# A two-layer mLSTM and windowed-attention trunk: filling order and rotation sums in attention, and the mLSTM gate chain, selectors, conditioning steps and latent squares, changed together

## The chip, the cores and the metric

The kernel runs on one core of a Trainium2 chip. A core has TensorE (PE in the profile; PEld is its weight load), VectorE (DVE), ScalarE (ACT), GpSimd (POOL) and SyncE (SP, which issues most DMAs here). Each engine works through its own instructions in order and waits for the others by semaphores. The metric is the time of one execution in microseconds (us) on the device.

## What is computed

Two layers of a trunk over 512 latent tokens and 256 context tokens, with 1024 features and float32 throughout. Both layers are modulated by linear maps of a conditioning vector (`mod_l`, `mod_c`). The reference, cut:

```python
for i in range(2):                      # layer 0: bidirectional mLSTM, layer 1: windowed attention
    mod_l = split(silu(c) @ ada_w[i] + ada_b[i], 6)      # mod_c the same from c_ctx
    u  = rms_norm(h,  norm_mix[i]) * (1 + mod_l[1]) + mod_l[0]      # uc from hc likewise
    y, yc = mlstm(uc, u) if i == 0 else attention(uc, u)
    h = h + mod_l[2] * y
    h = h + mod_l[5] * (relu(modulated_norm(h) @ w1[i]) ** 2 @ w2[i])
    # layer 0 does the same for the context stream hc
return rms_norm(h, final_norm)
# mlstm: gates -> log_i, log_sigmoid(log_f); per direction, in 128-token chunks:
b = cumsum(lf); m = running max of (m + lf, li); weights exp(...) from b, li, m
# attention: rope(q), rope(k); scores to 3 neighbouring blocks of 128 and to the context; softmax with a sink
```

## The kernel before

Every float32 product is made of three TensorE products (`mm3`, lines 93 to 98): each operand is split into a rounded part (`hi`, a copy on ACT, line 876) and the rest (`lo`, a subtraction, line 877, on DVE unless another engine is named). Weights come in units of 512 KB through a ring with three raw buffers (`unit`, line 74); `take` and `feed` keep the next ones ready.

The program is written with a tile framework. Its planner orders each engine's instructions by their place in the program and by when it reckons them ready, and places the waits. `keep_in_program_order` pins one instruction behind whatever was written before it for its engine. Fillers are Python generators: each `next` writes a few more instructions of other work at that place.

Layer 0. `layer0_mix` makes the gate logits and the first queries and keys. `gates` (line 576) is one generator: the chain of logarithms, four scans and three exponentials on DVE, ACT and POOL is written at its first `next`, ahead of `qk_out` and the values of the first head pair (`v_steps`, line 686); the second half, transposes on TensorE, follows after one and a half blocks of the output gate (`ogate`). Then `core` (line 725) runs for four head pairs, with the next pair's projections as filler. `new_es` (line 718) spreads selector columns for one pair; its product at line 740 begins a core, with the scaled keys `kp` (line 753). `ada_step` (line 249) is one conditioning step: a raw unit is loaded and multiplied with one or two conditioning rows on DVE (line 261, pinned). 80 such steps are spread over the layers: in `dense_steps`, in `v_steps` at j = 5, 1 and 3 of the order 4, 5, 0, 1, 2, 3, and elsewhere.

End of the mixer and feed-forward network of layer 0. `out_late` adds the mixer's output to `hC` and `hL`; `norm_add` (line 279) squares each of the eight blocks on ACT and adds the squares up on POOL, the last two on DVE. `norm_hooks` gives two hooks: `norm_rc` (line 300, sums over partitions on TensorE at line 307, then a power on POOL) and the normalisation itself. `plain` in `ffn0` (line 1008) does the first four hidden blocks, context before latent, with the latent's hooks after the first two context blocks. In the last round, `back` (line 1089) takes one block at a time, each in a bank of the pool `mm` (three banks; `at` has five).

Layer 1. `keys_begin` projects the context's keys and values, with the hooks of the latent norm inside. `rope` (line 1664) makes a rotation from three DVE products and one POOL sum (line 1677); `kv_out` and `q_out` split the result, and their `late` part transposes it on TensorE (lines 1702 and 1719) and copies it out. The attention loop runs over 16 tiles (g, j). In each, the string `PAT` sets the order: S is a quarter of a later tile's scores (`scores`, line 1726), T a turn of weights (line 1793, evacuated at lines 1798 and 1799), V a product with the values, F one filler step. The fillers (line 1541) come in the order: the late parts of the tile before, four key-value projection steps, four query steps, output projections. They and the turns share the pool `pt` (three banks).

Of the kernel before, what the change touches and what calls it, by code (L numbers as in the profile page):

```python
# [9 lines left out]
F32 = mybir.dt.float32  # L10
# [11 lines left out]
P = 128  # L22
# [34 lines left out]
class Trunk:  # L57
# [222 lines left out]
    def norm_add(self, st, g, kt, h, eng=None, temp=None, apart=False):  # L280
# [5 lines left out]
        elif kt:  # L286
            sq = self.np.tile([P, n], F32, name="sq", tag=f"sq{n}", bufs=2)
        else:
            sq = self.np.tile([P, n], F32, name=f"ss{g}", tag=f"ss{n}", bufs=1 if n == 512 else 2)
# [10 lines left out]
    def norm_rc(self, st, g):  # L300
# [4 lines left out]
        for j in range(nb):  # L305
            for i, acc in enumerate(st[g]):
                nc.tensor.matmul(out=ps[:, j:j + 1], lhsT=acc[:, j * P:(j + 1) * P], rhs=self.ones, start=i == 0,
                                 stop=i == len(st[g]) - 1)
# [43 lines left out]
    def layer0_mix(self):  # L352
# [79 lines left out]
        with tc.tile_pool(name="ml", bufs=1, reuse_waits="tile") as ml:  # L432
# [81 lines left out]
    def out_late(self, yu):  # L514
# [23 lines left out]
        for g in "CL":  # L538
# [3 lines left out]
            for n, m in enumerate((6, 7, 0, 1, 2, 3, 4, 5)):  # L542
# [8 lines left out]
                self.norm_add(self.st, g, n, self.out_add(m, g, t), nc.vector if n > 5 else None)  # L551
# [5 lines left out]
    def norm_hooks(self, g):  # L557
# [9 lines left out]
        return [lambda: x.append(self.norm_rc(st, g)), whole]  # L567

    def gates(self, psc, psl):
# [21 lines left out]
        with tc.tile_pool(name="gt", bufs=1, reuse_waits="tile") as gt:  # L591
# [33 lines left out]
            nc.gpsimd.tensor_tensor(out=t1[R], in0=li, in1=b, op=ALU.subtract)  # L625
# [20 lines left out]
            nc.scalar.activation(out=az, in_=az, func=AF.Exp)  # L646
# [4 lines left out]
            nc.scalar.activation(out=t1[64:104], in_=aa, func=AF.Exp)  # L651
            nc.scalar.activation(out=t2, in_=m, func=AF.Exp, scale=-1.0)
# [34 lines left out]
    def v_steps(self, p, v, rows, w=None):  # L687
        w = w or [self.take() for i in range(2)]
        for j in (4, 5, 0, 1, 2, 3):
# [9 lines left out]
            if p and j % 2:  # L699
# [18 lines left out]
    def new_es(self, p):  # L718

        self.es = self.mc.tile([104, 2, P], F32R, name="es", tag="es", bufs=2)  # L720
# [204 lines left out]
    def ffn0(self, hooks, done, pre):  # L925
# [82 lines left out]
        def plain(hid):  # L1008

            ws = [self.begun.pop(0) for _ in range(4)]  # L1010
            pools = [("mm", self.mm)] * 3 + [("at", self.at)]
            for g in "CL":
                xs = self.xs(self.u0)
                for m in range(4):
                    hi, lo = ws[m]
                    n = xs[g](0)[0].shape[-1]
                    ps = pools[m][1].tile([P, 512], F32, name="mm", tag=pools[m][0])[:, :n]
                    for kt in range(KT):
                        sl = slice(kt * P, (kt + 1) * P)
                        self.mm3(ps, hi[:, sl], lo[:, sl], *xs[g](kt), kt == 0, kt == KT - 1)  # L1020
                    r = r_tile(n)
                    nc.scalar.activation(out=r, in_=ps, func=AF.Relu)
                    nc.scalar.activation(out=r, in_=r, func=AF.Square)
                    if g == "C":
                        self.split(r, *[x[:, P:H] for x in hid[m][1]])
                        if m < 2:
                            hooks[m]()
                    else:
                        self.split(r[:, 0:H], *hid[m][0])
                        self.split(r[:, H:NL], *[x[:, 0:P] for x in hid[m][1]])  # L1030
                        self.feed()
                        if m % 2:
                            blocks(m // 2)
                        if m == 1:
                            self.ada_until(0, 5)
# [53 lines left out]
        def back(c, todo, hid, w, late=False):  # L1089
# [30 lines left out]
        for _ in range(2):  # L1120
            self.feed(True)
# [851 lines left out]
```

## Time and profile before

| | us |
|---|---|
| time, median of 3 runs (1566.23 to 1571.36) | 1568.58 |
| profiled execution, its own time | 1573.33 |
| its span | 1571.5 |
| PE / PEld busy | 1519.8 / 1365.5 |
| DVE / ACT / POOL busy | 1123.5 / 744.2 / 341.3 |

The span runs from the first to the last instruction of the profiled execution. Matmuls overlap, so a busy TensorE is not one at its peak. [...]

### The profile page before, as it was taken

The numbers are of one execution on the slowest core, as the hardware profiler recorded it, in microseconds if no ns is written. First come the engines' busy times: TensorE is split into PE (matmuls) and PEld (weight loads), VectorE is DVE, ScalarE is ACT, GpSimd is POOL, SyncE is SP. The second block draws the span as 40 slices with busy tenths as digits, with TensorE's granted clock in tenths as the row PEclk, the third lists the DMA queues.
The fourth block names the chain that finished last, engine by engine and source line by source line (L and its number), as shares of the span: only waits on it lengthen the run. The fifth ranks groups of instructions, "written<-read, shape, count | busy, mean of one in ns | idle before, by whom it ended". The sixth has DMA issues, their size and how long they took to land.

```text
span 1571.5 us, 23851 instructions
## 1 busy us (share of the span) xinstructions
PE 1519.8 (97%) x9110; PEld 1365.5 (87%) x9110; DVE 1123.5 (71%) x2064; ACT 744.2 (47%) x1506; POOL 341.3 (22%) x333
## 2 busy tenths in 40 slices
PE   7989999999999999999999999899999999999998
PEld 5778888878889999999999999788887888888886
DVE  3666556478777797876776668777888785767687
ACT  4534343334473533424325255566666665545454
POOL 0221111112213222233223322354443100000000
PEclk9989999999999999999999999999999999999999
DMA  8323223234321343343443421011101424150321
GB/s 311 131 74 108 94 95 94 79 101 138 101 68 67 105 136 123 133 148 119 149 135 120 134 81 66 23 41 41 41 28 55 157 82 151 40 170 32 107 68 54
DMA packets 47849, 157.28 MB, mean 100 GB/s; under 512 B 5327, under 2 KB 8911, under 8 KB 47607
## 3 DMA queue, kind: packets, MB, share of 16 engines
q1 hardware_dynamic: 46560, 154.25, 29.4%
q8 instruction: 72, 1.18, 0.3%
q10 hardware_dynamic: 1175, 1.51, 0.3%
q14 instruction: 42, 0.34, 0.1%
HBM read 153.64 MB, written 2.10 MB: 99 GB/s over the span
## 4 chain that ended last, share of the span: by engine, by line
PE 71%; DVE 8%; issue 6%; POOL 5%; ACT 4%; DMA 1%; POOLq 0%; DVEq 0%; ACTq 0%
PE mm L96 16%; PE mm L97 16%; PE mm L98 16%; DVE adap L261 2%; PE p L98 2%; PE p L96 2%; PE p L97 2%; PE pt L1793 1%; PE pj L96 1%; PE pj L98 1%; PE pj L97 1%; DVE wlo L877 1%; PE at L832 1%; ACT whi L876 1%; PE av L1809 1%
## 5 line engine op out<-in xcount | busy, mean ns | idle before, releaser
L877 DVE TENSOR_TENSOR wlo<-raw,whi 128x1024 fp32r<-128x1024 f32 (+2 forms) x152 | 182.6, 1205 | 87.9 <-ACT whi L876 87.1
L876 ACT CAST whi<-raw 128x1024 fp32r<-128x1024 f32 (+2 forms) x155 | 154.0, 1000 | 139.1 <-PE mm L97 74.7
L96 PE MATMUL mm<-uH,whi 128*128 128x512 f32 (+1 forms) x496 | 191.4, 390 | 3.9 <-ACT v L698 3.9
L97 PE MATMUL mm<-uL,whi 128*128 128x512 f32 (+1 forms) x496 | 188.8, 382 | 0.4 <-DVE uL L331 0.4
L98 PE MATMUL mm<-uH,wlo 128*128 128x512 f32 (+1 forms) x496 | 188.9, 382 | 0.0
L261 DVE SCALAR_TENSOR_TENSOR adap<-raw,crow 128x1024 bf16<-128x1024 f32 x128 | 167.0, 1305 | 21.6 <-DMA raw<-ada 20.8
L96 PE MATMUL mm<-h,whi 128*128 128x384 f32 x512 | 173.7, 339 | 4.0 <-DVE hL L1110 2.2
L97 PE MATMUL mm<-h,whi 128*128 128x384 f32 x512 | 172.9, 338 | 0.5 <-DVE h L877 0.5
L98 PE MATMUL mm<-h,wlo 128*128 128x384 f32 x512 | 172.6, 337 | 0.0
L96 PEld LDWEIGHTS mm<-uH,whi 128*128 128x128 f32 x496 | 94.0, 191 | 19.8 <-ACT v L698 4.2
L876 ACT CAST whi<-sum 128x512 fp32r<-128x512 f32 (+1 forms) x42 | 31.8, 760 | 166.3 <-PE mm L97 76.4
L98 PEld LDWEIGHTS mm<-uH,wlo 128*128 128x128 f32 x496 | 94.5, 191 | 17.9 <-issue 0.3
L97 PEld LDWEIGHTS mm<-uL,whi 128*128 128x128 f32 x496 | 94.6, 191 | 17.0 <-issue 1.0
L96 PEld LDWEIGHTS mm<-h,whi 128*128 128x128 f32 x512 | 96.4, 188 | 5.2 <-ACT h L876 2.6
L97 PEld LDWEIGHTS mm<-h,whi 128*128 128x128 f32 x512 | 96.4, 188 | 1.3 <-DVE h L877 1.2
L98 PEld LDWEIGHTS mm<-h,wlo 128*128 128x128 f32 x512 | 96.5, 188 | 0.0
L877 DVE TENSOR_TENSOR wlo<-wb,whi 128x1024 fp32r<-128x1024 f32 x49 | 59.2, 1222 | 35.9 <-ACT whi L876 35.8
L877 DVE TENSOR_TENSOR h<-r,h 128x384 fp32r<-128x384 f32 (+2 forms) x100 | 56.6, 568 | 35.4 <-ACT h L876 35.2
L876 ACT CAST whi<-wb 128x1024 fp32r<-128x1024 f32 x49 | 51.6, 1054 | 60.9 <-PE mm L97 27.1
L98 PE MATMUL p<-t,wlo 128*128 128x384 f32 x224 | 75.4, 337 | 0.3 <-DVE wlo L877 0.3
L97 PE MATMUL p<-t,whi 128*128 128x384 f32 x224 | 75.2, 336 | 0.0
L96 PE MATMUL p<-t,whi 128*128 128x384 f32 x224 | 75.2, 336 | 0.0
(396 smaller groups left out, 4175.2 us busy)
## 6 DMA issues: line engine op xcount, KB each, us to landing
raw<-ada SPq DMA_DIRECT2D x80, 512.0 KB, 3.5
raw<-w SPq DMA_DIRECT2D x64, 512.0 KB, 3.5
raw<-w2a SPq DMA_DIRECT2D x32, 512.0 KB, 3.5
wb<-w2b SPq DMA_DIRECT2D x28, 512.0 KB, 3.6
adaw<-ada SPq DMA_DIRECT2D x16, 512.0 KB, 5.7
hL<-xT SPq DMA_DIRECT2D x16, 256.0 KB, 3.7
raw<-wqk SPq DMA_DIRECT2D x8, 512.0 KB, 4.0
raw<-wv SPq DMA_DIRECT2D x8, 512.0 KB, 3.5
```

The costliest lines, as they stand in the source:

```text
L96: mm(out=out, lhsT=ah, rhs=bh, start=start, stop=False)
L97: mm(out=out, lhsT=ah, rhs=bl, start=False, stop=False)
L98: mm(out=out, lhsT=al, rhs=bh, start=False, stop=stop)
L261: self.tc.keep_in_program_order(nc.vector.scalar_tensor_tensor(out=pr, in0=w, scalar=0.5, in1=self.crow[:, v, :], op0=ALU.mult, op1=ALU.mu ...
L832: mm(out=o[hh][:, i * VW:(i + 1) * VW], lhsT=pw[g, d, hh][:, i, :], rhs=v[:, 3 * g + i, hh, :], start=False, stop=i == 2)
L876: keep(self.nc.scalar.copy(out=hi, in_=src))
L877: keep((eng or self.nc.vector).tensor_tensor(out=lo, in0=src, in1=hi.bitcast(F32), op=ALU.subtract))
L1793: nc.tensor.transpose(out=pt[:, i * P:(i + 1) * P], in_=ps_[i][:, n * P:(n + 1) * P], identity=self.ident)
L1809: mm(out=o, lhsT=vv, rhs=pl, start=False, stop=n == len(blks) - 1)
```

## The change

Twelve edits, none of which alters a result:

- `dense_steps`: the two blocks of the first output gate, whose `lo` is made on POOL, no longer make a conditioning step each; the same steps come later.
- `gates`: the one addition of the chain on POOL (line 625) goes to DVE; a `yield` behind it splits the chain, so that its second half is written after `qk_out` and `v_steps`; its three exponentials are pinned.
- `new_es(0)` is written before the first output gate.
- `v_steps`: conditioning steps at j = 4, 5, 0.
- Latent squares in `out_late`: blocks 0 to 3 are summed on POOL, 4 to 7 on DVE in a second tile, then both are added. The sum products of line 307 are pinned there.
- `plain`: the latent's hooks come after two context blocks and in the middle of the third; the fourth weight unit is split only then; latent blocks go in pairs, their first halves interleaved.
- `back`, last round: single blocks take `mm` and `at` in turn.
- `keys_begin`: the second hook comes one and a half steps later.
- `rope`: the sum is on DVE ahead of the loop and on POOL in the loop.
- `filler`: two projection steps, then the late parts (queries first), then the rest.
- `split_y`: the `lo` subtraction goes from POOL to DVE.
- `scores`: the maximum and the bias of the first tile are pinned.

```diff
@@ dense_steps
-                    self.ada_step()
+                    if not eng:
+                        self.ada_step()
@@ norm_add
-            sq = ...(name=f"ss{g}", tag=f"ss{n}", bufs=1 if n == 512 else 2)
+            sq = ...(name=f"ss{g}", tag=f"ss{n}", bufs=2)
@@ norm_rc
+    def norm_rc(self, st, g, keep=lambda i: i):
+                keep(nc.tensor.matmul(out=ps[:, j:j + 1], ...))
@@ layer0_mix
             for _ in self.v_steps(0, qkv[2], rows, wv):
                 pass
+            next(gt)
...
+            self.new_es(0)
             so = self.ogate(0, xs, nc.gpsimd)
...
-                self.new_es(0)
@@ out_late, norm_hooks
+                    self.norm_add(self.st, "DL"[n < 4], n % 4, x, nc.vector if n > 3 else None)
+                    if n == 7:
+                        s0, s1 = self.st["L"][0], self.st["D"][0]
+                        nc.vector.tensor_tensor(out=s0, in0=s0, in1=s1, op=ALU.add)
...
+        return [lambda: x.append(self.norm_rc(st, g, self.tc.keep_in_program_order)), whole]
@@ gates
-            nc.gpsimd.tensor_tensor(out=t1[R], in0=li, in1=b, op=ALU.subtract)
+            nc.vector.tensor_tensor(out=t1[R], in0=li, in1=b, op=ALU.subtract)
+            yield
+            keep = tc.keep_in_program_order
...
+            keep(nc.scalar.activation(out=az, in_=az, func=AF.Exp))
...
+            keep(nc.scalar.activation(out=t1[64:104], in_=aa, func=AF.Exp))
+            keep(nc.scalar.activation(out=t2, in_=m, func=AF.Exp, scale=-1.0))
@@ v_steps
-            if p and j % 2:
+            if p and j in (4, 5, 0):
                 self.ada_step()
@@ new_es
-        self.es = self.mc.tile([104, 2, P], F32R, ...)
+        self.es = self.ml.tile([104, 2, P], F32R, ...)
@@ ffn0, plain
+            for m in range(4):
+                ps = begin("C", m)
+                part("C", m, ps, 0)
+                if m == 2:
+                    hooks[1]()
+                part("C", m, ps, 1)
+                if m == 1:
+                    hooks[0]()
+                    self.feed(True)
+                    ws.append(self.begun.pop())
+            for i in range(2):
+                pss = [begin("L", 2 * i + m) for m in range(2)]
+                for kt in range(4):
+                    for m in range(2):
...
+                        self.mm3(pss[m], hi[:, sl], lo[:, sl], *xs("L", kt), kt == 0, False)
+                for m in range(2):
+                    part("L", 2 * i + m, pss[m], 1)
+                    self.feed()
@@ ffn0, back and the start
-                        pool, tag = (self.at, "at") if len(pss) % 2 else (self.mm, "mm")
+                        pool, tag = (self.at, "at") if (len(pss) + turn) % 2 else (self.mm, "mm")
...
-        for _ in range(2):
-            self.feed(True)
+        self.feed(True)
...
-                    back(c, [(t, m)], hid, ws)
+                    back(c, [(t, m)], hid, ws, turn=m)
@@ keys_begin
-                    if j == 4 and pr == 0 and i % 2:
-                        hooks[i // 2]()
+                    if j == 4 and (pr, i) in ((0, 1), (1, 0)):
+                        hooks[pr]()
@@ layer1_mix, filler
+                    its = chain(kv_steps(n) if n < 4 else (), q_steps(), out_steps(2 if n < 14 else 6))
+                    for _ in range(2):
+                        next(its, None)
+                        yield
+                    for f in fs[::-1]:
                         f()
                         yield
+                    yield from its
@@ split_y
-                nc.gpsimd.tensor_tensor(out=lo, in0=ys[g][:, i, :], in1=hi.bitcast(F32), op=ALU.subtract)
+                nc.vector.tensor_tensor(out=lo, in0=ys[g][:, i, :], in1=hi.bitcast(F32), op=ALU.subtract)
@@ rope
-        nc.gpsimd.tensor_tensor(out=t1, in0=t1, in1=t2, op=ALU.add)
+        eng.tensor_tensor(out=t1, in0=t1, in1=t2, op=ALU.add)
@@ scores
+                keep = self.tc.keep_in_program_order if g + j == 0 else lambda x: x
+                keep(nc.vector.reduce_max(out=mx, ...))
+                keep(nc.vector.scalar_tensor_tensor(out=nb[:, i0:i0 + per], ...))
```

## Rows read from the trace of the kernel before

**Rows 1.** The page: busy time of each engine; clock granted in 40 slices.

```profile
PE 1519.8 (97%) x9110; PEld 1365.5 (87%) x9110; DVE 1123.5 (71%) x2064; ACT 744.2 (47%) x1506; POOL 341.3 (22%) x333
...
PEclk9989999999999999999999999999999999999999
```

**Rows 2.** Stretches: start:end, length, busy us (instructions), granted clock, DMA share, GB/s.

```profile
92.74:99.57 6.83, 5.97 (x14) 4.72 (x15) 2.78 (x4) 4.63 (x8) 4.58 (x3) 0.50 0.00 0
338.49:345.33 6.84, 6.84 (x36) 4.13 (x35) 4.09 (x8) 1.76 (x5) 0.00 (x0) 0.50 0.41 146
437.49:444.32 6.83, 6.83 (x33) 6.83 (x33) 3.11 (x6) 2.09 (x6) 1.02 (x1) 0.50 0.50 158
949.49:952.90 3.41, 3.41 (x14) 3.41 (x13) 3.37 (x4) 1.68 (x3) 3.33 (x2) 0.50 0.04 5
990.45:993.86 3.41, 3.41 (x18) 3.13 (x18) 1.44 (x2) 0.00 (x0) 0.00 (x0) 0.50 0.00 0
1075.78:1079.20 3.42, 3.42 (x16) 2.98 (x15) 2.80 (x9) 1.86 (x6) 0.01 (x1) 0.50 0.01 2
1250.00:1500.00 250.00, 250.00 (x1114) 207.37 (x1113) 175.94 (x224) 135.20 (x185) 0.00 (x0) 1.00 0.31 103
```

**Rows 3.** Waits of PE: who waited for whom, us in total, times, longest.

```profile
PE mm L96 <- ACT v L698: 3.9, 1, 3.9
PE pt L1702 <- DVE ksp L1695: 3.8, 4, 1.5
PE pt L1719 <- DVE qsp L1714: 3.4, 4, 1.7
PE at L740 <- DVE kp L753: 3.3, 2, 1.7
PE mm L96 <- DVE hL L1110: 2.2, 1, 2.2
...
PE at L307 <- DVE ssL L294: 1.8, 1, 1.8
PE at L740 <- issue: 1.8, 1, 1.8
```

**Rows 4.** Timeline of ACT, 91 to 98 us: start, us, instruction, idle before.

```profile
91.15 1.28 ACT L652 ACT_TABLE_LOAD   x1 [9.72 <-DVE m L622]
...
96.82 0.84 ACT L651 ACTIVATE t<-aa 40x768 f32<-40x768 f32 x1 [1.58 <-DVE aa L650]
```

**Rows 5.** Timeline of DVE, 77 to 97 us.

```profile
77.55 2.52 DVE L261 SCALAR_TENSOR_TENSOR adap<-raw,crow 128x1024 bf16<-128x1024 f32 x1 [2.18 <-DMA raw<-ada]
...
81.26 0.94 DVE L616 SCALAR_TENSOR_TENSOR gz<-gz,aa 40x768 f32<-40x768 f32 x1
...
95.84 0.95 DVE L650 TENSOR_TENSOR aa<-t,ae 40x768 f32<-40x768 f32 x1 [1.74 <-POOL ast L642]
```

**Rows 6.** The stretch ahead of the third core's scaled keys, columns as above.

```profile
251.50:263.70 12.20, 11.66 (x90) 11.00 (x89) 11.99 (x20) 3.11 (x9) 4.82 (x4) 1.00 0.47 139
```

**Rows 7.** Timeline of DVE at 435 us.

```profile
435.36 1.49 DVE L294 TENSOR_TENSOR ssL<-ssL,sq 128x512 f32<-128x512 f32 x2 [2.32 <-POOL ssL L294]
```

**Rows 8.** The stretch at the end of layer 0, columns as above.

```profile
935.70:955.50 19.80, 17.58 (x102) 17.26 (x100) 19.49 (x29) 11.21 (x19) 9.08 (x5) 0.91 0.25 83
```

**Rows 9.** Timeline of DVE, 991 to 995 us.

```profile
991.46 1.23 DVE L1759 TENSOR_REDUCE mx<-s 128x2 f32<-128x1024 f32 x1 [1.15 <-PE s L1754]
...
994.79 0.28 DVE L1761 SCALAR_TENSOR_TENSOR nb<-mx,nsink 128x2 f32<-128x2 f32 x2
```

**Rows 10.** Timelines of POOL and of DVE, 1056 to 1060 us.

```profile
1056.71 2.54 POOL L1616 TENSOR_TENSOR y<-yT,y 128x512 fp32r<-128x512 f32 x2
...
1057.11 2.28 DVE L1695 TENSOR_TENSOR ksp<-rp,ksp 128x128 fp32r<-128x128 f32 x2 [0.68 <-ACT ksp L1694]
```

**Rows 11.** Evacuation of a turn, lines 1798 and 1799: ns min/median/max, first and last start.

```profile
L1798 ACT CAST ph<-pt x72: 573/587/632, 1001.5 to 1213.0; 128x512 fp32r<-128x512 f32 x72
...
L1799 DVE TENSOR_TENSOR pl<-pt,ph x72: 669/684/693, 1002.5 to 1213.7; 128x512 fp32r<-128x512 f32 x72
```

More of the change, by code (lines that the diff above doesn't have):

```diff
@@ L288, in norm_add @@
         else:
-            sq = self.np.tile([P, n], F32, name=f"ss{g}", tag=f"ss{n}", bufs=1 if n == 512 else 2)
+            sq = self.np.tile([P, n], F32, name=f"ss{g}", tag=f"ss{n}", bufs=2)
         nc.scalar.activation(out=sq, in_=h, func=AF.Square)
@@ L306, in norm_rc @@
             for i, acc in enumerate(st[g]):
-                nc.tensor.matmul(out=ps[:, j:j + 1], lhsT=acc[:, j * P:(j + 1) * P], rhs=self.ones, start=i == 0,
-                                 stop=i == len(st[g]) - 1)
+                keep(nc.tensor.matmul(out=ps[:, j:j + 1], lhsT=acc[:, j * P:(j + 1) * P], rhs=self.ones, start=i == 0,
+                                      stop=i == len(st[g]) - 1))
         rs = self.np.tile([P, 4], F32, name="rs", tag="rs", bufs=2)[:, 0:nb]
@@ L718, in new_es @@
     def new_es(self, p):
-        self.es = self.mc.tile([104, 2, P], F32R, name="es", tag="es", bufs=2)
+        self.es = self.ml.tile([104, 2, P], F32R, name="es", tag="es", bufs=2)
         self.nc.gpsimd.tensor_copy(out=self.es.rearrange("r d (h e) -> r d h e", e=64),
@@ L1008, in plain @@
         def plain(hid):
-            ws = [self.begun.pop(0) for _ in range(4)]
+            ws = self.begun
+            self.begun = []
             pools = [("mm", self.mm)] * 3 + [("at", self.at)]
[L1012 to L1018, printed above, removed]
-                        sl = slice(kt * P, (kt + 1) * P)
[L1020 to L1035, printed above, removed]
@@ new lines, in xs, with begin, part @@
+            def xs(g, kt):
+                return self.xs(self.u0)[g](kt)
+            def begin(g, m):
+                n = xs(g, 0)[0].shape[-1]
+                return pools[m][1].tile([P, 512], F32, name="mm", tag=pools[m][0])[:, :n]
+            def part(g, m, ps, half):
+                hi, lo = ws[m]
+                for kt in range(4 * half, 4 * half + 4):
+                    sl = slice(kt * P, (kt + 1) * P)
+                    self.mm3(ps, hi[:, sl], lo[:, sl], *xs(g, kt), kt == 0, kt == KT - 1)
+                if not half:
+                    return
+                r = r_tile(ps.shape[-1])
+                nc.scalar.activation(out=r, in_=ps, func=AF.Relu)
+                nc.scalar.activation(out=r, in_=r, func=AF.Square)
+                if g == "C":
+                    self.split(r, *[x[:, P:H] for x in hid[m][1]])
+                else:
+                    self.split(r[:, 0:H], *hid[m][0])
+                    self.split(r[:, H:NL], *[x[:, 0:P] for x in hid[m][1]])
@@ L1086, in seven, with back @@
                 self.feed(True)
-        def back(c, todo, hid, w, late=False):
+        def back(c, todo, hid, w, late=False, turn=0):
             pss = {}
@@ L1491, in layer1_mix @@
                 f()
-            kvl = [self.kv_out(sw, 0, j, pss[j]) for j in range(4)]
+            kvl = [self.kv_out(sw, 0, j, pss[j], nc.vector) for j in range(4)]
             late = []
@@ L1497, in layer1_mix @@
                     self.proj_part(wq[0], j, rows, 256, i, ps)
-                late.append(self.q_out(sw, 0, j, ps))
+                late.append(self.q_out(sw, 0, j, ps, nc.vector))
                 for f in kvl[2 * j:2 * j + 2]:
@@ L1516, in kv_steps @@
                         yield
-                    late.append(self.kv_out(sw, 1, j, ps))
+                    late.append(self.kv_out(sw, 1, j, ps, nc.gpsimd))
                 def q_steps():
@@ L1529, in q_steps @@
                         yield
-                    late.append(self.q_out(sw, g, j, ps))
+                    late.append(self.q_out(sw, g, j, ps, nc.gpsimd))
                 def out_steps(n):
@@ L1535, in out_steps, with filler @@
                             yield from parts.pop(0)()
-                def late_steps(fs):
-                    for f in fs:
+                def filler(n):
+                    fs, late[:] = late[:], []
+                    its = chain(kv_steps(n) if n < 4 else (), q_steps(), out_steps(2 if n < 14 else 6))
[3 more added lines that the diff above has]
+                    for f in fs[::-1]:
                         f()
                         yield
-                def filler(n):
-                    fs, late[:] = late[:], []
-                    its = [late_steps(fs), q_steps(), out_steps(2 if n < 14 else 6)]
-                    if n < 4:
-                        its.insert(1, kv_steps(n))
-                    for it in its:
-                        yield from it
+                    yield from its
                 curs = [[] for _ in todo]
@@ L1687, in kv_out @@
         if j < 4:
-            k = self.rope(sw, j, ps[:, 0:128], 2)
+            k = self.rope(sw, j, ps[:, 0:128], 2, eng)
         else:
@@ L1706, in kv_out, with q_out @@
         return late
-    def q_out(self, sw, g, j, ps):
+    def q_out(self, sw, g, j, ps, eng):
         nc = self.nc
         qs = self.swd["qs"]
-        q = self.rope(sw, j, ps, 4)
+        q = self.rope(sw, j, ps, 4, eng)
         sp = sw.tile([P, 4, 2, DH], F32R, name="qsp", tag="sp", bufs=4)
```

30 lines of the change are left out of this document (16 added, 14 removed).

## The prediction

> **What bounds the kernel now.** I read the page first, then the stretches, then the waits of PE, and only then the timelines of the places that these name. The page shows PE busy for 97% of the span, DVE 71%, ACT 47% and POOL 22% [rows 1]. So TensorE sets the time, and no edit takes a product away from it. What can be won is what it loses. [...] In the late dense stretch 1114 products start in 250 us, one in 0.224 us, at the full clock [rows 2]: nothing is to be won there. [...]
>
> **The change part by part**, each with the value that I take and its bounds.
>
> (a) *Gate chain.* At 91.15 ACT takes up the exponential of line 652, which the planner put ahead of three copies of values; the engine had been idle for 9.72 us until then, with PE's banks full behind it [rows 4]. PE waits 3.9 us [rows 3], and the clock is low for 6.83 us afterwards, a loss of 3.4 [rows 2]. Pinned behind the copies of `v_steps`, the exponentials can't hold them up. What is late next? PE goes on from about 89.4 with the output gate's first block, 24 products of 512 columns and 24 of 256, at 0.224 and at least half of that: 8.1 us, until 97.5. Then it needs the chain. That ends today with line 651 at 97.66 [rows 4]. The third exponential now comes behind it (+0.84, as line 651), the addition that leaves POOL adds a DVE operation (+0.95, as line 650), and the two conditioning products that stood before line 616 go, which is worth between nothing and 3.7 us (81.26 less 77.55) [rows 5]. The chain ends between 95.7 and 99.5: PE waits for up to 2 us or not at all. The addition also waits on DVE behind the scans, so its price is inside that sum. The pause at line 740 (1.8 us, no releaser named) [rows 3] comes behind a copy out of a bank as well; I count 0.7 of it, because the two conditioning loads that go make room in the ring. Value 3.9 + 3.4 + 0.7 = 8.0; bounds 2 (a wait of 2 us, and the clock falls all the same) and 9.1.
>
> (b) *Conditioning steps and selectors.* For 12.2 us ahead of the third core DVE is busy for 11.99, mostly with four conditioning steps, and the scaled keys queue behind them [rows 6]; PE waits 3.3 us in two such places, and after the second the clock is low for 6.84 us (3.4) [rows 2, 3]. The change moves the last of three steps ahead by three value blocks, some 2.5 us of DVE. The trace does not show that its load can come earlier (each needs one of three raw buffers). Value 2, of 0 to 6.7. The two steps that (a) drops run later, among other DVE work; `new_es(0)` is one POOL copy and is hidden by the output gate.
>
> (c) *Latent squares.* DVE stood idle for 2.32 us for POOL's serial sums and then needed 1.49 us for two of its own [rows 7]. Four sums on DVE take 3.0, beside POOL's three: the chain ends about 2.32 − 1.5 = 0.8 us earlier. The pinned sums also stand behind two context blocks, where one was written ahead of them; as the planner may have moved them already, this covers between nothing and 24 products of 256 columns, 2.7 us by half of 0.224 us each; I take 0.5. Of the wait of 1.8 us [rows 3] 1.3 go, and of the low clock behind it (6.83 us, 3.4) [rows 2] one half, 1.7, as the power on POOL and its transposes still follow. Value 3, of 0 to 5.2.
>
> [...]
>
> (d) *Last round of `back`.* PE waits 2.2 us for a bank of `mm`, and the clock is low for 3.41 us after it (1.7) [rows 2, 3]. With `at` in turn there are more banks. But DVE is busy for 19.49 of 19.80 us there [rows 8]: what PE gains, the sums of the latent norm may ask back, as they end when DVE does. Value 1.5, of 0 to 3.9.
>
> (e) *Attention.* The first tile's bias (line 1761) is computed at 994.79, though its maximum ended at 991.46 + 1.23 = 992.69 [rows 9]: pinned, it saves up to 2.1 us of the pipeline's start. The transposes of lines 1702 and 1719 cost 7.2 us in eight waits [rows 3], and two low-clock stretches (3.41 and 3.42 us, 3.4 lost) lie beside them [rows 2]. Now 12 projection products come ahead of the late parts, over 1.3 us by half of 0.224 us each, about the mean wait of 0.9. `split_y` no longer holds POOL for 2.54 us a pair, and DVE's splits lose that neighbour [rows 10]; in exchange DVE gets six subtractions of 0.68 (as line 1799) [rows 11]. The rotation sums ahead of the loop go from POOL to DVE. No row has that form on DVE; bounds are nothing and 0.68 (line 1799, twice as wide) [rows 11]. I take 0.4, nearer to the middle, as it replaces a hand-over between engines. Value: two thirds of 7.2, half of 3.4 and nothing for the bias: 6.5, of 0 to 12.7.
>
> **The sum.** 8 + 2 + 3 + 1.5 + 6.5 = 21 us. Every edit also makes the planner lay out the stages behind it anew; for that I take off one new wait of 1.8 us with a third of the usual 3.4: 3 us. Net 18. The upper bounds give 9.1 + 6.7 + 5.2 + 3.9 + 12.7 = 37.6, the lower ones 2 − 3 = −1. Against the profiled execution (1573.3, with a span of 1571.5) this is 1555.3; that run lies 4.7 above the median, and the same gain taken from the median of 1568.6 gives 1550.6, so 1551.
>
> **The rivals.**
>
> *Only the pins work.* The planner places by its own reckoning, and the stages where DVE is full (b, c, d) or the late parts are merely renamed stay as they are. Then (a) gives its 8 and the rest what a new wait takes: 1561, within 1557 to 1566. For it: DVE at 11.99 of 12.20 and 19.49 of 19.80 [rows 6, 8]. Against it: the waits of rows 3 have different causes, so they would not all stay.
>
> *The change doesn't do what it says.* The planner puts the instructions into the old order, as most edits only move them in the program. Then the time is 1568. Against it: the exponentials, the first bias and the latent sums are pinned.
>
> *Slower: the banks of `pt`.* A projection now holds one of three banks while the late parts transpose through another. A turn's bank is free only after ACT's 0.587 and DVE's 0.684 us [rows 11]. If PE then meets a bank not yet emptied once a tile, it waits 1.27 us in each of 14 tiles, 17.8 us, and three low-clock stretches like 1075.78 (1.7 each) add 5.1. With (a) to (d) at 14.5 less 3, that is 1568.6 − 11.5 + 22.9 = 1580. It decides from the point where less than 1.27 us of other products stands between two turns. Against it: today a projection holds its bank across three turns too, and the view of waits shows no such wait of PE in the loop.
>
> [...]
>
> **How the numbers follow.** Forecast 0.61 (1544 to 1561), the clock 0.08 (1538 to 1546), only the pins 0.20, the old order 0.05, banks 0.06. The range reaches from 1538, between the forecast and the sum of all upper bounds (1531), to 1565, which leaves out the old order, the banks and 0.07 of the others: 0.18. A measurement of this kernel can tell 0.3% (4.7 us) from no change. Faster than 1563.9: the forecast, the clock and 0.14 of the pins, 0.83; within: 0.11; slower: 0.06.
>
> **What would show it.** Right: no wait of PE on ACT's copy of values, no low-clock stretch around 95 or 440 us, the first transposes of the gates before 100 us; the waits at lines 1702 and 1719 under 3 us; FFN stages as long as now. Wrong: a new wait at lines 657 or 740 of over 2 us (a), sums of line 307 waiting on DVE for as long as now (c, d), turns of line 1793 waiting for line 1799 (banks), or low-clock stretches that are as long in sum as the present 30.7 us.

## The result, and the profile after

The changed kernel takes **1550.4 us** (median; 1549.05 to 1557.02), the kernel before 1569.8 in the same comparison: a ratio of 0.989, 95% interval 0.987 to 0.9911, or 19.4 us less. The forecast was 1551. The profiled execution of the changed kernel took 1551.29 us with a span of 1549.4, which is 22.0 below the profiled one of before.

The page, as in [rows 1]: busy time of each engine, and the granted clock in 40 slices (PEclk: the share of TensorE's full clock that was granted, in tenths). The clock is called low where the granted share is 0.50; in the dense stretch of [rows 2] it is 1.00.

```profile
PE 1509.6 (97%) x9110; PEld 1355.9 (88%) x9110; DVE 1127.1 (73%) x2084; ACT 740.2 (48%) x1501; POOL 326.5 (21%) x318
...
PEclk8999999999999999999999999999999999999999
```

The number of products is the same, 9110, and so is PE's share; DVE has 20 instructions more and POOL 15 fewer. The waits of PE answer to [rows 3] (who waited for whom, us in total, times, longest):

```profile
PE s L1778 <- ACT e L1798: 2.2, 3, 0.8
PE at L308 <- DVE ssL L295: 2.1, 1, 2.1
...
PE mm L96 <- ACT y L1655: 2.0, 1, 2.0
...
PE at L751 <- DVE kp L764: 1.8, 2, 1.1
...
PE at L751 <- ACT tok L670: 1.7, 1, 1.7
...
PE pt L1750 <- DVE qsp L1745: 0.5, 1, 0.5
PE pt L1825 <- DVE hL L1680: 0.5, 1, 0.5
...
PE pt L1750 <- DVE pl L1831: 0.5, 2, 0.2
```

The changed kernel has more lines, so lines 307, 740, 1702, 1719 and 1793 of before are 308, 751, 1733, 1750 and 1825 here. ACT's copy of the values (3.9 us before) is gone as a cause, the transposes of keys and queries fell from 7.2 us to 0.5 (as a wait for DVE's splits), the scaled keys from 3.3 to 1.8. The wait for the latent sum is still there with 2.1 us; what the reader must look up is its time: it is at 938 us now, at the end of layer 0, and no longer at 435. The low-clock stretches behind 60 us that hold products, as in [rows 2] (start:end, length, busy us of each engine, granted clock, DMA share, GB/s):

```profile
425.79:429.20 3.41, 3.25 (x15) 3.25 (x16) 2.10 (x4) 0.72 (x1) 0.10 (x1) 0.50 0.68 204
941.20:948.03 6.83, 6.54 (x31) 6.25 (x31) 3.74 (x7) 1.44 (x3) 1.82 (x5) 0.50 0.12 48
```

That is 10.2 us in place of 30.7 (the six stretches at 0.50 in [rows 2] together), or of 34.1 with a stretch of 3.41 us at 109.81 us that [rows 2] does not list. A third stretch, of 10.24 us at 26 us, lies in the loading phase: with it the first stage below took 70.0 us, and 69.3 in the second execution, which has none there.

Where the time went is read best by stages. Each number below is the time between the starts of two products in the timeline of PE, in us (the first row counts from the start of the span); the columns are the profiled executions of the kernel before, the changed one and a second execution of it (x11), and of five of the kernels below.

| stage, up to the start of | before | changed | x11 | x1 | x2 | x5 | x9 | x12 |
|---|---|---|---|---|---|---|---|---|
| last product of the gate logits and first queries and keys | 72.0 | 70.0 | 69.3 | 72.8 | 69.5 | 69.4 | 71.1 | 68.8 |
| first selector product (line 740) | 36.9 | 29.8 | 29.7 | 29.9 | 30.6 | 29.7 | 29.7 | 27.6 |
| the same of the second core | 80.1 | 79.4 | 80.0 | 79.2 | 79.9 | 80.0 | 79.4 | 79.2 |
| of the third | 71.8 | 71.9 | 71.9 | 71.8 | 71.8 | 71.8 | 71.8 | 71.8 |
| of the fourth | 73.6 | 72.1 | 72.3 | 75.3 | 72.2 | 76.9 | 72.1 | 72.1 |
| context sums of layer 0 (line 307) | 84.8 | 81.8 | 81.8 | 85.3 | 81.8 | 85.3 | 81.8 | 81.8 |
| first `p` product of `ffn0` that reads `t` | 88.1 | 87.0 | 86.0 | 88.3 | 85.5 | 87.0 | 85.8 | 86.0 |
| last `p` product | 403.9 | 404.3 | 404.0 | 404.7 | 403.8 | 405.3 | 406.0 | 403.3 |
| first latent projection of layer 1 | 55.0 | 56.3 | 56.2 | 55.7 | 56.3 | 56.2 | 56.2 | 56.0 |
| first score product | 23.4 | 22.0 | 22.1 | 23.4 | 22.0 | 22.1 | 22.1 | 22.1 |
| last product with the values | 226.1 | 219.0 | 219.0 | 223.2 | 225.8 | 219.0 | 219.0 | 218.7 |

What follows to the end takes 355.8 us in both kernels.

### The profile page after: what moved, and what is told of

Same layout as the page of the kernel before. It is cut to its first block, busy times and chain, and to the rows that moved or that the text cites. A ratio compares the mean times of both kernels' runs of the same rounds, so it can differ in the third digit from the quotient of the medians.

```text
span 1549.4 us, 23838 instructions
## 1 busy us (share of the span) xinstructions
PE 1509.6 (97%) x9110; PEld 1355.9 (88%) x9110; DVE 1127.1 (73%) x2084; ACT 740.2 (48%) x1501; POOL 326.5 (21%) x318
## 4 chain that ended last, share of the span: by engine, by line
PE 79%; DVE 6%; issue 4%; ACT 4%; POOL 3%; DMA 1%; POOLq 0%; DVEq 0%; ACTq 0%
PE mm L96 17%; PE mm L97 16%; PE mm L98 16%; PE p L98 2%; PE p L97 2%; PE p L96 2%; PE pt L1825 2%; PE pj L96 1%; PE pj L97 1%; PE pj L98 1%; PE at L843 1%; DVE adap L262 1%; PE av L1840 1%; ACT whi L887 1%; DVE wlo L888 1%
## 5 line engine op out<-in xcount | busy, mean ns | idle before, releaser
L888 DVE TENSOR_TENSOR h<-r,h 128x384 fp32r<-128x384 f32 (+2 forms) x100 | 56.4, 568 | 34.1 <-ACT h L887 33.8
L1809 POOL TENSOR_SCALAR e<-e,den 128x512 f32<-128x512 f32 (+1 forms) x64 | 49.0, 779 | 135.1 <-DVE den L1807 86.9
L97 PE MATMUL p<-t,whi 128*128 128x384 f32 x224 | 75.2, 336 | 0.0
```

Of the source, the lines that this page charges most:

```text
L97: mm(out=out, lhsT=ah, rhs=bl, start=False, stop=False)
L888: keep((eng or self.nc.vector).tensor_tensor(out=lo, in0=src, in1=hi.bitcast(F32), op=ALU.subtract))
L1809: nc.gpsimd.tensor_scalar(out=out[ii][:, :W], in0=out[ii][:, :W], scalar1=den[:, ii:ii + 1], scalar2=1.0, op0=ALU.mult, op1=ALU.mult)
```

## The experiments

**x1, part (a) alone.** The kernel before with the gate edits:

```diff
+                    if not eng:
+                        self.ada_step()
+            next(gt)
+            self.new_es(0)
+            nc.vector.tensor_tensor(out=t1[R], in0=li, in1=b, op=ALU.subtract)
+            yield
+            keep(nc.scalar.activation(out=az, in_=az, func=AF.Exp))
```

> The kernel before with part (a) alone: gate chain in two parts with pinned exponentials, its addition on DVE, the two conditioning steps of the first output gate dropped, the first selectors written earlier. Theory (each part works by the waits at its own place): the first selector product comes at 99.8 us from the start in place of 108.9, as in the changed kernel, and nothing else goes: the third core's two waits for the scaled keys (1.8 us each), the low clock of 3.4 us behind the second, the latent sum's wait (2.0) and its low clock stay. Time 1569.8 - 9.1 - 0.7 = 1560. Rival (the gains belong to the new plan as a whole, not to the parts): the places behind are laid out anew too, and the time falls by over 13 us, under 1557, or by under 5.

Measured: 1564.6 us (ratio 0.9965, 0.9946 to 0.9985). Counted from the first row of the table the second core begins 7.8 us earlier (29.9 + 79.2 against 36.9 + 80.1), the same as in the changed kernel, so this part stands by itself. The first selector product came at 102.7 us all the same, not at 99.8, since the first stage took 72.8 us. The time fell by 5.4 us only, between the 10 of the theory and the 5 of the rival; the profiled execution in the table, at 1569.3, is one of the slowest of eight (1561.15 to 1569.35). The waits that part (a) leaves alone are as long as before, but the low clock behind them is another, and what the other stages gave and took by that is seen in the table (third to fourth core +1.7, attention loop -3.0, and +2.2 behind it):

```profile
258.15:261.56 3.41, 3.41 (x14) 1.62 (x12) 3.39 (x6) 0.43 (x2) 0.00 (x0) 0.50 0.51 145
333.25:340.08 6.83, 6.83 (x36) 4.17 (x35) 4.13 (x8) 1.89 (x6) 0.00 (x0) 0.50 0.40 134
432.23:439.06 6.83, 6.83 (x34) 6.83 (x34) 3.13 (x5) 2.48 (x6) 1.02 (x1) 0.50 0.47 157
1213.89:1220.72 6.83, 6.83 (x34) 6.80 (x33) 2.74 (x7) 2.31 (x5) 1.44 (x2) 0.50 0.00 0
```

The first and the last of these have no counterpart in [rows 2], although the waits ahead of them (at the third core, and for the attention's output) are in the kernel before too; the two inside the attention of [rows 2] are missing here.

**x5, part (b) undone.**

```diff
-            if p and j in (4, 5, 0):
+            if p and j % 2:
```

> The changed kernel with part (b) undone: conditioning steps behind the value blocks 5, 1 and 3 again. Theory (the steps' new places close the waits for the scaled keys): from the third to the fourth core's first selector product 73.6 us in place of 72.1, and from there to the context's sums 84.85 in place of 81.80, with 6.8 us of low clock behind the wait, as in the kernel before: 4.5 us more. Rival (the squares and the first part did it): 72.1 and 81.8 as in the changed kernel. Besides: the last gate product came 2.0 us earlier in the changed kernel (70.0 against 72.0), but at 72.8 in the kernel with part (a) alone; if that belongs to (b) it is at 72 here, if to the squares' buffers at 70.

Measured: 1560.1 us in one execution. PE's waits between 240 and 420 us, and the two stretches behind them, of this kernel:

```profile
PE at L751 <- DVE kp L764: 3.4, 2, 1.8
```

```profile
256.55:263.38 6.83, 6.83 (x29) 4.63 (x27) 3.81 (x7) 1.48 (x3) 0.00 (x0) 0.50 0.33 121
331.65:338.48 6.83, 6.83 (x36) 4.22 (x35) 3.87 (x9) 1.32 (x4) 0.00 (x0) 0.50 0.45 152
```

Both waits are back, and the low clock behind each: 4.8 us to the fourth core and 3.5 to the context sums, 8.2 in all where 4.5 were expected. The first of the two stretches has no counterpart in [rows 2], so part of the excess is the clock. In the changed kernel one wait of 1.1 us is left there, and the clock stays up:

```profile
326.80:333.60 6.80, 6.79 (x54) 4.52 (x55) 6.23 (x15) 1.58 (x6) 0.00 (x0) 1.00 0.40 120
```

The first stage took 69.4 us here too, so it does not belong to (b).

**x9, part (c) undone.**

```diff
-                    self.norm_add(self.st, "DL"[n < 4], n % 4, x, nc.vector if n > 3 else None)
+                self.norm_add(self.st, g, n, self.out_add(m, g, t), nc.vector if n > 5 else None)
...
-            ws = self.begun
+            ws = [self.begun.pop(0) for _ in range(4)]
```

> The changed kernel with part (c) undone: the latent squares' sums in one chain, the sums of line 307 not pinned, the first four hidden blocks in the old order, two weight units ahead. Theory (c gives what the trace shows): from the context's sums to the first p product 88 us in place of the changed kernel's 87.0 (3.4 us of low clock in it) and of 85.5 in the five runs with (c) and without low clock there; PE waits about 2 us for the latent sum. Besides, the start: the last gate product came at 69.4 to 70.7 us in all eight kernels that have (c), and at 72.0 and 72.8 in the two without: here at 72 if it belongs to (c). Rival: 85.5 to 87 us, so that (a) and (b) ahead of it did it, and 70 us at the start.

Measured: 1552.5 us in one execution, and 85.8 us for the stage, in the rival's range; the wait for the latent sum came as the theory says. Its waits between 400 and 432 us, and those of the changed kernel:

```profile
PE at L308 <- DVE ssL L295: 1.8, 1, 1.8
PE at L321 <- POOL rc L313: 0.4, 1, 0.4
```

```profile
PE at L321 <- POOL rc L313: 1.1, 1, 1.1
...
PE at L308 <- DVE ssL L560: 0.2, 1, 0.2
```

The sum's wait of 1.8 us does go with (c), to 0.2, and 0.7 us of it come back one instruction later, as a wait for POOL's power (`rc`, 0.4 to 1.1), which stands between the sum and the transposes. Without low clock the stage is 85.8 us here and 85.5 in the five kernels that have (c) (x2 among them); with a stretch of 3.41 us in it, as in the changed kernel and x11, it is 86.0 to 87.0. The 88.1 of before hold 6.83 us of low clock [rows 2] behind the same wait, which x9 does not show. The start (71.1) lies between the two values expected; to which part the 1 to 3 us of the first stage belong stays open.

**x3, the turn of banks undone** (part d, with the hook of the key projections).

```diff
-                        pool, tag = (self.at, "at") if (len(pss) + turn) % 2 else (self.mm, "mm")
+                        pool, tag = (self.at, "at") if len(pss) % 2 else (self.mm, "mm")
```

> The changed kernel with the turn of banks in the last round of the feed-forward network and the later hook in the context's key projections undone. The stage from the last product of the second-last weights (p, 896 us) to the first latent projection (952.5) was 1.7 us longer in the changed kernel than before (56.3 against 54.6 us). Theory 1 (the turn moves the wait from the bank to the latent sum of line 308 and its low clock, a bad exchange): without it the stage is 54.6 us again and the time 1.7 us less, 1548.7. Theory 2 (the loss comes from elsewhere, the turn itself gains the 2.2 us of the bank's wait): the stage gets 1 to 4 us longer still, 1551.4 to 1554.4.

Measured: 55.0 us for the stage, as theory 1 says, but 1554.9 us (0.9909, 0.989 to 0.9929), which it does not. The stage behind took 22.8 us in place of 22.0: from the last `p` product to the first score it is 77.8 against 78.3, and before it was 78.4. The waits between 890 and 975 us are merely elsewhere (and PE no longer waits for the sum):

```profile
PE mm L96 <- DVE hL L1144: 2.2, 1, 2.2
PE pt L1750 <- DVE qsp L1745: 1.1, 1, 1.1
```

In this trace the time is lost behind these stages: the attention loop took 220.5 us in place of 219.0, with 3.41 us of low clock at 974 us, and the rest to the end 357.3 in place of 355.8, with 3.41 us at 1199. x8 below, the other variant without the wait for the sum, has the same two stretches, 220.3 and 357.3 us. Whether they come from the edit or by chance is not shown.

**x4 and x8, the hooks of the latent norm later.**

```diff
-                    if j == 4 and (pr, i) in ((0, 1), (1, 0)):
+                    if j == 4 and (pr, i) in ((0, 3), (1, 2)):
```

and, in x8,

```diff
-                    if j == 4 and (pr, i) in ((0, 1), (1, 0)):
+                    if j == 5 and (pr, i) in ((0, 1), (1, 0)):
```

> The changed kernel with both hooks of the latent norm inside the context's key projections two projection steps (24 products of 256 columns, 2.8 us) later. Theory (the sum of line 308 stands too early in the program, PE waits 2.3 us for DVE's last sum, and the low clock of 6.83 us behind it comes from that pause): the wait goes, and with it 3.4 us of low clock: the stage is 50.6 to 52 us in place of 56.3, the time 1545. Rival (the norm is late whatever stands in front): the pause moves to the normalised blocks' first product and is as long, or the low clock comes all the same: 1549 to 1552.

> The changed kernel with the two hooks of the latent norm inside the second context block of the key projections (same steps, one block of 48 products later). Two projection steps were not enough: PE still made 36 products and then waited 2.2 us for DVE's last sum. Theory (the planner had put the sum behind 36 products already, so only a place behind more than that moves it; 60 products end about when the sum is ready): no wait at line 308, no low clock behind it, the stage from the last p product to the first latent projection is 52.5 to 54 us in place of 56.1 to 56.3, the time 2.5 to 3.7 us less than the changed kernel's 1550.4. Rival (the latent blocks are then late): PE waits for the first normalised latent block for as long as it gained, 56 us again.

Measured: x4 1550.6 us (0.9892, 0.9872 to 0.9911), with the same 36 products ahead of the sum and the same wait of 2.1 us; the edit moved nothing. x8 1553.8 us (0.9897, 0.9878 to 0.9917): its stage up to the first latent projection is 51.4 us, 4.9 less, and the next one 27.0, 5.0 more. Its waits between 890 and 976 us:

```profile
PE pt L1750 <- DVE qsp L1745: 1.5, 1, 1.5
PE pj L97 <- DVE wlo L888: 0.9, 2, 0.5
PE pt L1733 <- DVE ksp L1726: 0.9, 1, 0.9
PE s L1778 <- DVE qs L1753: 0.8, 1, 0.8
```

No wait at the sum any more, and in its place a row of waits for DVE. The rival holds for the two stages together: what PE gained it lost, though later than the rival said. In all these kernels, before, changed, x1 to x9, the two stages together take 77.8 to 79.1 us, whatever PE waits for on the way, so the place of PE's wait does not decide them. That DVE's work does is likely, as most of these waits are for DVE, but not shown. These two stages of the changed kernel (columns as in [rows 2]):

```profile
896.30:974.60 78.30, 74.24 (x501) 72.63 (x499) 57.72 (x131) 40.36 (x88) 16.41 (x17) 0.96 0.20 65
```

DVE is busy for 57.72 of the 78.30 us; it is full only in some 15 us ahead of the sum.

**x2, x6 and x7: attention.** x2 undoes all of part (e), x6 the order of the fillers alone, x7 the rests of the output alone.

```diff
-                    for _ in range(2):
-                        next(its, None)
-                        yield
-                    for f in fs[::-1]:
+                    for f in fs:
```

and, in x7,

```diff
-                nc.vector.tensor_tensor(out=lo, in0=ys[g][:, i, :], in1=hi.bitcast(F32), op=ALU.subtract)
+                nc.gpsimd.tensor_tensor(out=lo, in0=ys[g][:, i, :], in1=hi.bitcast(F32), op=ALU.subtract)
```

> The changed kernel with part (e) undone: the old order of the fillers, the rotation sums and the attention output's rests on POOL, the first bias not pinned. Theory: the stretch from the first latent projection of layer 1 to the last product with the values is 8.5 us longer, 249.5 us in place of 241.0, with the waits of the key and query transposes (7.2 us) and two stretches of low clock back: 1550.4 + 8.5 = 1559. Rival (the attention gained from what comes before it, the latent norm's new end): under 3 us longer, under 1553.5.

> The changed kernel with the attention loop's old filler order alone (late parts first, keys before queries). From the first score product to the last product with the values it took 219.0 us in the changed kernel and 225.8 with all of part (e) undone, 3.4 of that by two low-clock stretches. Theory (the order is what closes the waits of the transposes): 222 to 223 us without low clock, waits of the key and query transposes over 4 us in sum. Rival (POOL's two subtractions per pair, beside which DVE's splits run long, are the cause): under 220 us, waits under 2 us.

> The changed kernel with the attention output's rests on POOL again, everything else as changed. By the theory that the filler order does it: the loop takes 219 to 219.5 us, and the two 128x128 splits of a pair of keys beside POOL's subtraction may run to 2.3 us without PE waiting for them. By the rival that the neighbour on POOL does it: 221 us or more, with PE waiting for the key splits by over 1 us at 1040.

Measured: x2 1556.5 us (0.9923, 0.9906 to 0.994), x6 1557.1 and x7 1554.6 in one execution each. From the first score to the last product with the values they take 225.8, 221.5 and 222.8 us against 219.0 (x2 loses 6.8 of the 8.5 us expected there); 225.8 holds two low-clock stretches of 3.4 us and 222.8 one. The waits between 970 and 1200 us, of x6:

```profile
PE pt L1747 <- DVE qsp L1742: 4.0, 4, 2.1
PE pt L1730 <- DVE ksp L1723: 2.2, 2, 1.4
PE pt L1822 <- DVE hL L1677: 1.9, 2, 1.0
```

and of x7:

```profile
PE s L1778 <- ACT e L1798: 4.1, 5, 2.2
```

The longest of these, 2.19 us at 1043.56, hangs on a query split, in the timelines of ACT and of DVE in x7:

```profile
1041.05 0.41 ACT L1744 CAST qsp<-rp 128x256 fp32r<-128x256 f32 x1 [0.95 <-POOL rp L1708]
```

```profile
1041.49 1.03 DVE L1745 TENSOR_TENSOR qsp<-rp,qsp 128x256 fp32r<-128x256 f32 x1 [0.66 <-ACT qsp L1744]
```

With the old order alone the transposes' waits are back (6.2 us). With the rests on POOL they stay away, but PE waits 4.1 us for banks of scores in place of 2.2. The query split in front began late, as POOL's rotation sum queued behind POOL's first subtraction and ACT waited 0.95 us for it, and it took 1.03 us on DVE beside POOL's second, 0.41 without. So the time is the rival's, but not the wait that it named. Two causes, each worth some 2 to 2.7 us, each from one execution. Waits for a bank of `pt` are few: a turn waits for an output projection's bank (line 1822, 1.9 us in x6; 0.5 in the changed kernel), and the query transposes for a turn's (0.5 in the changed kernel). Of x2's two stages before the loop the second is 22.0 as in the changed kernel: the 1.4 us that keys and queries won ahead of the loop do not come from (e).

**x10 and x12, three and two more places.** x10 makes three edits more (the third moves three small copies to POOL besides the query units shown); x12 makes the first two alone.

```diff
+                    self.pin = bool(eng and m)
                     w[m] = self.take(eng)
+                    self.pin = False
...
-            addg(w7, s1, s7)
+            (addg if m0 == 0 else add)(w7, s1, s7)
...
-            wq = {0: [self.unit(a["wsq"][0, i]) for i in range(2)]}
+            wq = {0: [self.unit(a["wsq"][0, i], nc.gpsimd) for i in range(2)]}
```

> The changed kernel and three further edits, each at a place where a wait is left. First: the split of the weight unit that follows the gates is pinned, so that ACT copies the gate columns (line 670) before it takes up a unit whose load has not landed (2.6 us idle, PE waits 2.0 at line 751). Second: in the later of two seven-product blocks the sum w7 is on DVE (0.55) in place of POOL (1.68), ahead of PE's wait of 1.9 us. Third: the rests of the two query weight units and three small copies ahead of the attention loop are on POOL, which is idle there, 3.1 us off DVE. Theory (DVE is the bound from the last round to the first score): the last p product to the first score product takes 76 us in place of 77.8 to 78.4, and the first two places give 2.0 and 1.1: 5 us in all, 1545.5, and the low clock comes less often. Rival (each wait is replaced by the next in line): under 2 us, 1548.5 to 1552.

> The changed kernel with the first two of the three further edits: the pinned split of the weight unit that follows the gates, and the sum w7 of the later seven-product blocks on DVE. In the run with all three these two took 2.1 us (first gate product to first selector product, 27.6 against 29.7) and 1.0 us (403.0 against 404.0 in the stage of the p products) off, and the third gave 4.8 us back ahead of the first score product. Theory (waits at distant places add): both gains stay, the last p product to the first score product is 78.3 us as in the changed kernel, and the time is 1549.8 - 3 = 1546.8. Rival (what PE gains early it loses to the next wait): 1549 to 1551.

Measured: x10 1552.5 us (0.9899, 0.9882 to 0.9916), x12 **1547.4** (0.9862, 0.9838 to 0.9887; 1546.0 to 1549.57). The first edit gives 2.1 us (27.6 against 29.7) and the second 0.5 to 1.3 (403.0 and 403.3 against 403.8 to 404.3 without low clock at 650 us), in both kernels. The third lost 4.8 us in the stage ahead of the first score (26.9 against 22.1), or 3.1 from the last `p` product on (81.4 against 78.3, where 76 were expected), and the timelines of DVE and of POOL in x10 show how (start, us, instruction):

```profile
955.00 4.78 DVE L1728 TENSOR_TENSOR ksp<-rp,ksp 128x128 fp32r<-128x128 f32 x2 [1.34 <-ACT ksp L1727]
```

```profile
954.85 4.78 POOL L890 TENSOR_TENSOR wlo<-raw,whi 128x1024 fp32r<-128x1024 f32 x2 [17.41 <-ACT whi L889]
```

Two key splits that take 0.28 us each elsewhere lasted as long as POOL's two subtractions beside them, 2.4 us each, and PE waited 3.3 us for the keys. The rests were off DVE, and DVE spent 4.78 us on two splits beside them all the same. x12 is the best of these kernels, as its theory said (1546.8): 2.4 to 3.0 us under the two medians of the changed one, where the intervals still overlap.

**x11, the changed kernel once more.**

> The changed kernel once more, to have it beside the one with three more places on the same chip, and to see which low-clock stretches a second execution of the same program shows. Theory (a pause makes the low clock likely, not certain): the same waits to 0.2 us, but other low-clock stretches than at 426 and 941 us, and a time of 1549 to 1557. Rival (the program fixes them): low clock at the same two places and nowhere else after 60 us.

Measured: 1549.8 us (1549.67 to 1559.27; ratio 0.9888, 0.9868 to 0.9909). The waits are the same but for two that are missing where its low clock runs (0.7 us at line 751, 1.1 at line 321). The low clock behind the two latent sums came again (at 423.49 and 938.90 us); the stretch of the loading phase is gone, and one at the first selector is new. So the theory holds in part, and the rival, which had nothing at a third place, does not. The first selector's stretch of this execution, and the same stretch of the first one:

```profile
99.22:102.63 3.41, 3.41 (x10) 2.92 (x10) 3.41 (x8) 0.65 (x5) 0.00 (x0) 0.50 0.60 179
```

```profile
99.22:102.63 3.41, 2.16 (x9) 1.67 (x10) 3.41 (x7) 1.42 (x7) 0.00 (x0) 1.00 0.47 142
```

## Why the prediction came out right, step by step

The sum was 18 us on the profiled execution and 22.0 came; between the medians 19.4. The size is right, and three of its terms are not. The five terms came to 20.6 us where 21 were forecast, as more in (b) and (e) made up for less in (c) and (d); that they meet so closely is luck. The 3.4 and 1.7 us that the terms take for low clock are an estimate, half of 6.83 and 3.41 us at a granted 0.50 [rows 2]; where the cost could be read it was 2.3 to 2.4 and 1.1 to 1.5 us (last section). Of the 22.0 us, 2.9 in (e) and 0.7 in (a) are low clock that the one execution happened to have and the other not.

**(a) Gate chain: 8 forecast, 7.8 measured.** The split and the pins did what the rows said: the last of the three exponentials now ends at 93.10 + 0.85 = 93.95 where the last one ended at 97.66 (2.0 of that is the shorter first stage), PE goes on to the transposes at 95.86 without a wait, and the low clock at 92.74 is gone. One step failed: of the pause at line 740 I counted 0.7 us as won by two loads fewer, and it is as long as before. Its cause is ACT, which stood 2.56 us in front of a weight unit whose load had not landed, with the gate columns behind it (the row names PE, but the load was issued at 94.49 us and took 3.3 us to land, until 97.8):

```profile
97.94 1.04 ACT L887 CAST whi<-raw 128x1024 fp32r<-128x1024 f32 x1 [2.56 <-PE at L761]
...
99.16 0.73 ACT L670 COPY tok<-at 128x416 f32<-128x416 f32 x2
```

x12 pins that unit behind the columns and gets 2.1 us. The 0.7 that did come, up to the second core, is the low clock behind that pause, which this execution happened not to have.

**(b) Conditioning steps: 2 forecast, 4.5 measured** (1.5 to the fourth core, 3.0 behind it; x5 loses 8.2 without it). The mechanism was right and the term too small: I took a third of its upper bound, since the trace of before could not show whether the loads would come in time for the earlier steps. They do, as one wait is closed and the other shorter (1.6 to 1.1), and the low clock, which I had counted in the upper bound alone, goes with them.

**(c) Latent squares: 3 forecast, 1.1 measured in this pair, and 0.3 between x9 and the kernels with (c) where neither has low clock.** The step that failed is what an earlier sum is worth: the wait at the sum fell by 1.6 us (x9), more than the 1.3 reckoned, but POOL's power and the transposes behind it are next, 1.1 us of them uncovered in place of 0.4, and of the 0.9 us that are left the stage shows 0.3. I had named them and charged them to the clock alone; and x9 has the wait of 1.8 us without any low clock behind it, so the 1.7 us taken for that hung on a draw. POOL's and DVE's sums did not run side by side: POOL's last ended at 418.30, DVE's first began at 418.68, so none of them could run long beside another, as the splits of [rows 10] do.

**(d) Last round: 1.5 forecast, nothing measured in its two stages.** The bank's wait of 2.2 us went and the latent sum's of 2.1 came, with 6.83 us of low clock in place of 3.41. The warning stood in the text (what PE gains, the sums ask back), and the value should have followed it: with DVE busy for 19.49 of 19.80 us [rows 8], closing a wait of PE there gave nothing. x3, x4 and x8 show that from three sides. What remains open is the time of the whole kernel: x3's median is 4.5 us above the changed one's, and its trace shows 3.0 us lost behind these stages, which is not explained.

**(e) Attention: 6.5 forecast, 7.1 measured in the loop.** The waits of lines 1702 and 1719 fell by 6.7 us, the two stretches of low clock are gone, and the loop without low clock is 3.4 to 4.2 us shorter (x2's 225.8 less 3.4, half the length of its two stretches at 0.50, and x1's 223.2, against 219.0). The other 2.9 us of the 7.1 are a draw: x1 has the loop of before without a low stretch in it. Both causes that were named carry it (x6, x7). `nb` was counted at nothing and was not tried by itself.

**The planner's share: 3 us taken off, none needed.** The one new wait, in (d), is already in its stage. The first stage gave 2 us that nothing forecast.

**The rivals.** Only the pins work: no, (b) and (e) gave more than half. The old order kept: no. Banks of `pt`: waits of the kind are there, but 1.0 us in all and not 17.8. The clock (0.08 of the chances, at 1538 to 1546): no run shows what that range needs, a clock that stays up; the low stretches come back behind the pauses that are left, in some executions and not in others (at the first selector 3.41 us in x11, none in the first execution). Of the signs set out beforehand all held but two: a low-clock stretch near 440 us is still there in the changed kernel (425.79), and the sum of line 307 waits for DVE again, at the end of layer 0.

## What to carry to other kernels

Judge a wait of TensorE by the engine that it waits for: where VectorE was full ahead of the wait, three ways of moving it (x3, x4, x8) left the two stages at 77.8 to 78.4 us, and where the work could go into idle time, a place three blocks earlier gave most of the wait and a pin gave all of it. Look one instruction behind a wait that is to go, for what is due next there. And measure a stage from product to product over several executions, since the low clock behind a pause can be a draw (3.41 us of it at the first selector in one of the two executions of the changed kernel) that a single trace shows as if it were fixed.

## What the runs showed of the hardware

**The low clock behind a pause is in part a matter of chance, and how often it comes differs by place.** The 14 traces are of 13 kernels; only the changed kernel was traced twice. At the first selector product, with a wait of about 2 us, the low clock followed in 8 of the 12 executions that have this wait; at 650 us, behind one of 1.7 to 1.8 us, in 5 of 12; at the wait for the attention's output (1.9 to 2.0 us) in 7 of 14; at the latent sum at the end of layer 0 (2.0 to 2.1 us) in 10 of 10. At the fourth core it followed in all three executions with a wait of 1.6 us and in none of the eleven with 1.1 to 1.2. At these places it lasted 3.41, 6.83 or 10.24 us. What it costs is seen where nothing else differs: from the last product with the values to the sums behind the output projection it was 13.9 us without, 15.0 to 15.4 with 3.41 us and 16.2 to 16.3 with 6.83 us of it. That is 1.1 to 1.5 and 2.3 to 2.4 us, less than the half of each that the forecast reckoned; why is not shown (PE's waits in there are 0.8 us in the changed kernel and 0.6 in x1 with its 6.83 us). x11 beside the first execution of the changed kernel shows low stretches that come and go: at 26 us (none and 10.24 us) and at the first selector (3.41 us and none).

**Splits on DVE ran long beside a subtraction on POOL.** Beside POOL's two subtractions of 128x1024, which took 4.78 us and had begun 0.15 us earlier, two subtractions of 128x128 on DVE took 4.78 us as well, 2.4 each in place of 0.28 (x10). Two of them took 2.28 us beside POOL's two of 128x512, 2.54 us long [rows 10], and one of 128x256 took 1.03 in place of 0.41 beside one of those (x7). So work moved from DVE to an idle POOL need not be off DVE; for other instructions than these it is not shown.
